# Sums of x in the projections, attention ahead of four products, stores on GpSimd, four embedding banks: one change to a hybrid decoder layer

## The chip, the cores and the metric

One core of one Trainium2 chip. The metric is the device time of one execution in microseconds (us); the median of repeated runs counts. The engines are named as in the profile: PE is TensorE (matmuls; PEld its weight loads), DVE is VectorE, ACT is ScalarE, POOL is GpSimd, SP is SyncE, which here only starts DMAs. "SPq" in a view is SP's queue of instructions, "PEclk" the granted share of TensorE's full clock.

## The reference

One layer with SEQ = 1024 tokens and D_MODEL = 2048, everything in fp32:

```python
h = rmsnorm(h_res, g_pre[i])
u = h @ w_in[i]
(gq, gk, gv, g_gate, g_lr, sq, sk, sv, s_gate) = jnp.split(u, offsets, axis=-1)
log_a = jax.nn.log_sigmoid(g_lr @ w_a2[i] + b_a[i]) / GLA_TAU
o_gla = gla_chunked(...)            # 4 heads, chunks of 64
o_gla = rmsnorm(o_gla, g_gla_head[i]) * jax.nn.silu(g_gate)
o_sb = stick_breaking(...)          # 8 heads, strictly causal
o_sb = o_sb * jax.nn.silu(s_gate)
mix = jnp.concatenate([o_gla, o_sb], axis=-1) @ w_out[i]
h_res = h_res + rmsnorm(mix, g_post[i])
gate = jax.nn.sigmoid(h_res @ w_ple_gate[i] + b_ple_gate[i])
h_res = h_res + gate * (p[i] @ w_ple_proj[i])
```

## The kernel before, in words

Everything lies transposed: features on the 128 partitions, tokens in two halves (hf 0 and 1) of 512. An fp32 product is made of three matmuls: each operand is split (lines 99 and 100) into a rounded high part and a low part, and hi·hi, lo·hi and hi·lo are added in one PSUM bank. High parts are made by ACT, low parts by DVE.

**Projections.** `dense` makes one unit of 128 columns of x·w_in for both halves: 16 k-steps of six matmuls, weights through `wload` (a load of 256 KB into one of two `raw` tiles, split into `hi` and `lo`, four tiles each). After each k-step `step()` advances generators, Python coroutines that hold the rest of the work cut into pieces: one piece of `urgent` (turning v by a DMA transpose), one of `beside`, and pieces of `jobs` at a rate (`rate[1]`). The jobs are here GLA's four heads (rate 1.0) and then the eight stick-breaking heads (rate 0.9). Results of projections lie in `u` tiles (12), attention's results go to DRAM, `o_d`. So the order of the work on each engine comes from where the generators are advanced, and from priorities (`tc.high_priority`), by which a scheduler draws loads and evictions forward.

**Tail.** The two gate columns of w_in (`w_gate`, silu's argument) aren't multiplied as a plain product but by a Strassen-Winograd scheme: seven products of halves in place of eight, with sums of x (S1 to S4), sums of weights and intermediate results (u, v). The first two of these products are made as 16 "small products" of 24 matmuls, through the same `raw` tiles, while attention's rest runs as `jobs`. The first eight (`keep_u1`) store their result in `u1_d`. The other eight (`gate_11`) load it again, load `o_d`, gate it and store `og_d`. Beside them, two generators in `beside`, `x_sets_2` and `x_sets_1`, make the sums of x that the next stage needs: they load quarters of x (`x_part`, 256 KB each), scale one by g_pre on ACT (L699), add or subtract on DVE (L700 and L714), split the sums S2 and S1 into PE's operands, and keep one sum for later (`sx_d`). The last `LAST_11` = 2 of the small products come after the attention pools have been closed, when the "mix" pool, whose tiles `wr` (4), `wh`, `wl` and `ar` (3 each) carry all that follows, has been opened.

**Wide stages.** From there blocks of eight "wide" products of 24 matmuls follow. In the loops, `wload2` loads 512 KB of weights into `wr` (L820), DVE makes sums of weights (L813, L816), `wsplit` splits them, and some weight sums are stored for a later stage (L992, L993; for w_out L1055, L1056). `staged` loads an operand into an `ar` tile (L802), `to_slot` splits it, and `fill` does that for a set. In order: S2 and S1 with sums of w_gate (16 products); x's second half (8); S3 (8), whose results `gate` turns into `og_d` of half 1; S4 (8), which does it for half 0, loading `o_d` for each pair of columns (L802) and storing `og_d` (L961). Then the same scheme for w_out: A11 (8), S2 and S1 (16), and so on, with the sums S1 to S4 of `og_d` made by `sums_12` (stores L879 and L884) and, during A11, by `last_sums`. Then the post norm, `stream` (which stores `h_d`), and the scheme once more for the embedding gate w_g, where `embed` makes two matmul groups of p·w_p into a PSUM bank of tag z (L1145 loads w_p), and `gated` (L1166 reads that bank) writes `out`.

All DMAs are started by SP, in the order in which it has them: an instruction that waits holds all behind it. PSUM's eight banks are dn 4, z 2, t 1, o 1. Tags t and o serve attention.

Of the kernel before, what the change touches and what calls it, by code (L numbers as in the profile page):

```python
# [18 lines left out]
P = 128  # L19
# [32 lines left out]
W = 2 * HT  # L52
KP = KT // 2
RATE_BG = 0.5
LAST_11 = 2


@with_exitstack
def layer(ctx, tc, xT, w_in, w_gate, w_lr, w_a2, b_a, g_pre, g_head, w_out, g_post,
# [64 lines left out]
    def part(t, k):  # L124
        return t[:, (k % 2) * HT:(k % 2 + 1) * HT]
# [22 lines left out]

    urgent, jobs, beside = deque(), deque(), deque()
    rate = [0.0, 0.0]  # L150

    def advance(queue):
        while queue:
# [100 lines left out]
    with tc.tile_pool(name="att", bufs=1, reuse_waits="tile") as ap:  # L254
# [379 lines left out]
        def low_rank(hf):  # L634
# [9 lines left out]
            A.activation(lrT[rows], z[rows], AF.Copy)  # L644
            V.tensor_tensor(lrT[rest], z[rest], f(lrT[rest]), op=ALU.subtract)

        rate[1] = RATE_GLA
# [35 lines left out]


        u1_d = [dram.tile([P, W], F32, name=f"u1_d{i}") for i in range(4)]
        sx_d = [dram.tile([P, W], F32, name=f"sx_d{i}") for i in range(4)]
        g_sets = {"S1": [], "S2": []}

        def g_of(k):
            return gpre_s[:, k:k + 1]  # L690

        def x_part(hf, k):
            t = at("u")
            dma2(t, part(xT[hf, k // 2], k))
            return t

        def x_sum(k):
            t, a = x_part(1, k + 8), x_part(1, k)
            A.activation(t, t, AF.Copy, scale=g_of(k + 8))  # L699
            V.scalar_tensor_tensor(t, a, g_of(k), t, op0=ALU.mult, op1=ALU.add)  # L700
            return t

        def x_set(name, hf, k, t, wides={}):
            if k % 2 == 0:
                wides[name] = act_wide(hf, k // 2)
            pair = tuple(part(x, k) for x in wides[name])
            split(*pair, t)
            g_sets[name].append(pair)

        def x_sets_2():  # L710
            for k in range(8):
                t, c = x_sum(k), x_part(0, k)
                yield 1
                V.scalar_tensor_tensor(c, c, g_of(k), t, op0=ALU.mult, op1=ALU.subtract)  # L714
                dma2(part(sx_d[k // 2], k), c)
                yield 1
                x_set("S2", 1, k, c)
                yield 1

        def x_sets_1():  # L720
            for k in range(8):
                t = x_sum(k)
                yield 1
                x_set("S1", 0, k, t)
                yield 1

        def small_product(a, src, evac):
            p = ps("dn")
# [45 lines left out]

    mp = ctx.enter_context(tc.tile_pool(name="mix", bufs=1, reuse_waits="tile"))
    late = [None]

    def mt(tag, bufs, n=W, dt=F32, name=None):
        pool = mp if tag in ("wr", "wh", "wl", "ar") else late[0]
# [6 lines left out]
    if True:  # L786
# [87 lines left out]
        def sums_12(rows, s1, s2):  # L874
            for i in rows:
                a, b, c = staged(og_d[0][i]), staged(og_d[0][i + 4]), staged(og_d[1][i])
                add(a, a, b)
                sub(c, c, a)
                dma2(s2_d[i], c)  # L879
                yield 1  # L880
                s2.append(to_slot(1, i, c))
                yield 1
                if s1 is None:
                    dma2(s1_d[i], a)  # L884
# [12 lines left out]
        rate[1] = RATE_BG  # L897

# [34 lines left out]
        def stream(hf, kp, c):  # L933
            x = staged(xT[hf, kp])
            for n in (2 * kp, 2 * kp + 1):
                V.scalar_tensor_tensor(part(c, n), part(c, n), gpost_s[:, n:n + 1], r[hf],
                                       op0=ALU.mult, op1=ALU.mult)
            add(c, c, x)
            dma2(h_d[hf][kp], c)
            yield 1  # L940


# [2 lines left out]
        def gate(n, hf, p, other):  # L945
# [15 lines left out]
            dma2(og_d[hf][n // 2], z)  # L961

        def times_g(t, kp):
            for k in (2 * kp, 2 * kp + 1):
                A.activation(part(t, k), part(t, k), AF.Copy, scale=g_of(k))

        def g_then(a, kp, b, op):
            for k in (2 * kp, 2 * kp + 1):
                V.scalar_tensor_tensor(part(a, k), part(a, k), g_of(k), part(b, k), op0=ALU.mult, op1=op)
            return a  # L970

        def make_x3(i):
            a, b = staged(xT[1, i]), staged(xT[0, i])
            times_g(b, i)
            return g_then(a, i, b, ALU.subtract)

        def make_x4(i):
            a, b = staged(xT[0, i + 4]), staged(sx_d[i])
            return g_then(a, i + 4, b, ALU.add)


        t2_d, t3_d = drams("g2_d", 8), drams("g3_d", 8)
# [2 lines left out]
        for j in range(8):  # L985
            with ahead():
                b11, t1, t2 = (wload2(w_gate[kh, nh, j]) for kh, nh in ((0, 0), (0, 1), (1, 1)))
                sub(t1, t1, b11)
                sub(t2, t1, t2)
                w2, w1 = wsplit(t2), wsplit(t1)  # L990
                add(b11, b11, t2)
                dma(t2_d[j], t2)  # L992
                dma(t3_d[j], b11)  # L993
            p = product(g_sets["S2"], w2)
            with soon():
                add(u(j), p, u(j))
            p = product(g_sets["S1"], w1)
            with soon():
                add(v(j), p, u(j))
        drain()  # L1000

        job(fill("S3", 1, make_x3))
        job(fill("S4", 2, make_x4))
        for j in range(8):
            with ahead():
                t4, t2 = wload2(w_gate[1, 0, j]), wload2(t2_d[j])
# [30 lines left out]
        for j in range(8):  # L1037
# [3 lines left out]
            with soon():  # L1041
                A.activation(u(j), p, AF.Copy)
                if j % 2:
                    dma2(m_d[j // 2], st_u[j // 2])
        drain()

        job(fill("S3", 0, both(og_d[0], og_d[1], sub)))
        for j in range(8):
            with ahead():
# [5 lines left out]
                dma(t2_d[j], t2)  # L1055
                dma(t3_d[j], b11)  # L1056
            p = product(sets["S2"], w2)
            with soon():
                add(u(j), p, u(j))
# [7 lines left out]
        for j in range(8):  # L1067
# [3 lines left out]
            with soon():  # L1071
# [2 lines left out]
                add(part(c, j), p, v(j))  # L1074
                add(u(j), p, u(j))
                if j % 2:
                    dma2(c_d[0][4 + j // 2], c)
                    squares(0, c)
        drain()

# [25 lines left out]
        for j in range(8):  # L1106
# [3 lines left out]
            with soon():  # L1110
# [1 line left out]
                    c = staged(m_d[j // 2])  # L1112
                add(part(c, j), p, part(c, j))
                if j % 2:
                    dma2(c_d[1][j // 2], c)
                    squares(1, c)
        drain()

# [9 lines left out]
        drain()  # L1128


        p_act, pw, res = {}, {}, {}

        def load_p(hf):
            raw = staged(pT[hf])
# [4 lines left out]
        def embed(n, hf):  # L1139
            def go():  # L1140
# [16 lines left out]
        def gated(n, hf, p, other, last=False):  # L1157
# [11 lines left out]
                dma2(part(out[hf, n // 2], n), t)  # L1169
            elif n % 2:  # L1170
                add(wide[key], wide[key], h)
                dma2(out[hf, n // 2], wide[key])

        def stream_1():
            norm(1)
# [43 lines left out]
        for j in range(8):  # L1219
            with ahead():  # L1220
# [4 lines left out]
                dma(t2_d[j], t2)  # L1225
            p = product(sets["S2"], w2)
            with soon():
                add(u(j), p, u(j))
# [101 lines left out]
```

## Time and profile before

| | |
|---|---|
| median of 3 runs | 2166.53 us (2165.53 to 2167.83) |
| the profiled execution | 2170.56 us |
| its span, first to last instruction | 2168.7 us |
| mean granted clock | 0.986 |
| busy PE, DVE, ACT, POOL | 2104.2, 1509.6, 882.5, 110.3 us |
| DMA | 354.92 MB, mean 164 GB/s |

Busy time is summed over an engine's instructions. In the groups and timelines an entry such as `dn<-ah,wh` is the output tile and the inputs, by the program's names; `L89 PE MATMUL` is the kernel's line, the engine and the operation. What stands after `<-` in an idle time is the engine, the tile and the line that ended it. A wait is put down to one releaser, the one that came last. The projections last until about 1115 us, the tail until 1244, the wide stages to the end.

### The profile page before, as it was taken

Reading aid. Unit: us, or ns where it says so; the run is one execution under the profiler, and the core shown is the slowest. Engines: PE = TensorE matmul, PEld = TensorE weight load, DVE = VectorE, ACT = ScalarE, POOL = GpSimd, SP = SyncE. Lnnn points to the kernel's source line nnn. Section 1 sums busy time; section 2 is a strip of 40 time slices with the busy share of each in tenths; the row PEclk is TensorE's granted clock in tenths of the full one; section 3 lists DMA queues with packets and bytes.
Section 4 is the critical chain, followed back from the end, with each engine's and each line's share of the span. In section 5 each row is a group of like instructions: output and inputs, shape, how many; then the busy total and the mean of one; then the engine's idle time right before and its main releaser. Section 6 shows DMA issues by size and latency. Waiting matters only on the chain.

```text
span 2168.7 us, 26868 instructions
## 1 busy us (share of the span) xinstructions
PE 2104.2 (97%) x9712; PEld 1716.6 (79%) x9712; DVE 1509.6 (70%) x2275; ACT 882.5 (41%) x1401; POOL 110.3 (5%) x228
## 2 busy tenths in 40 slices
PE   9999999999999999999999699999799999999998
PEld 6788888888888888888887588887588888778887
DVE  8557676666766666666677777886677787785765
ACT  7333333333455555544556323333233434322332
POOL 3000000000001110110100000000000000000000
PEclk9999999999999999999999899999799999999999
DMA  6212222221233334333359888778887686786763
GB/s 204 72 51 59 59 56 58 59 59 49 58 88 83 80 81 94 81 78 86 85 162 261 273 317 287 250 255 303 290 306 244 219 294 218 261 284 224 235 202 123
DMA packets 229669, 354.92 MB, mean 164 GB/s; under 512 B 124448, under 2 KB 129440, under 8 KB 229536
## 3 DMA queue, kind: packets, MB, share of 16 engines
q1 hardware_dynamic: 229536, 353.21, 51.9%
q8 instruction: 76, 1.25, 0.2%
q14 instruction: 57, 0.47, 0.1%
HBM read 257.19 MB, written 68.68 MB: 150 GB/s over the span
## 4 chain that ended last, share of the span: by engine, by line
PE 72%; DMA 13%; DVE 9%; issue 4%; ACT 2%; SPq 1%; DVEq 0%; POOL 0%; ACTq 0%
PE dn L89 63%; PE z L89 5%; DMA wr<-w_g 3%; PE t L89 2%; PE o L89 2%; DVE wl L100 2%; DMA u<-xT 1%; DMA E<-X 1%; DVE ev L813 1%; DMA ar<-og_d 1%; DMA og_d<-ev 1%; DMA xraw<-xT 1%; DMA ar<-xT 1%; DMA ar<-h_d 1%; DMA wr<-w_out 1%
## 5 line engine op out<-in xcount | busy, mean ns | idle before, releaser
L89 PE MATMUL dn<-ah,hi 128*128 128x512 f32 x1408 | 569.1, 404 | 0.2 <-ACT u L662 0.2
L89 PE MATMUL dn<-al,hi 128*128 128x512 f32 x1408 | 557.8, 396 | 0.3 <-DVE al L226 0.3
L89 PE MATMUL dn<-ah,lo 128*128 128x512 f32 x1408 | 557.8, 396 | 0.0
L89 PE MATMUL dn<-ah,wh 128*128 128x512 f32 x1216 | 478.1, 393 | 32.6 <-ACT ah L99 19.4
L89 PE MATMUL dn<-ah,wl 128*128 128x512 f32 x1216 | 476.7, 392 | 0.0
L89 PE MATMUL dn<-al,wh 128*128 128x512 f32 x1216 | 476.3, 392 | 0.1
L89 PEld LDWEIGHTS dn<-ah,hi 128*128 128x128 f32 x1408 | 265.8, 189 | 65.5 <-issue 2.8
L89 PEld LDWEIGHTS dn<-al,hi 128*128 128x128 f32 x1408 | 265.3, 188 | 65.4 <-DVE al L226 1.2
L89 PEld LDWEIGHTS dn<-ah,lo 128*128 128x128 f32 x1408 | 266.1, 189 | 54.3
L89 PEld LDWEIGHTS dn<-ah,wh 128*128 128x128 f32 x1216 | 230.5, 190 | 83.9 <-ACT ah L99 20.8
L99 ACT ACTIVATE wh<-wr 128x1024 fp32r<-128x1024 f32 x152 | 159.1, 1055 | 294.0 <-PE dn L89 140.1
L89 PEld LDWEIGHTS dn<-al,wh 128*128 128x128 f32 x1216 | 230.1, 189 | 50.1 <-DVE al L100 2.0
L89 PEld LDWEIGHTS dn<-ah,wl 128*128 128x128 f32 x1216 | 230.6, 190 | 48.4
L100 DVE TENSOR_TENSOR wl<-wr,wh 128x1024 fp32r<-128x1024 f32 x152 | 184.5, 1219 | 11.7 <-ACT wh L99 11.4
L99 ACT ACTIVATE hi<-raw 128x512 fp32r<-128x512 f32 x192 | 120.3, 627 | 154.8 <-PE dn L89 151.7
L100 DVE TENSOR_TENSOR lo<-raw,hi 128x512 fp32r<-128x512 f32 x192 | 133.7, 698 | 58.6 <-ACT hi L99 58.2
L305 ACT ACTIVATE X<-E 128x256 uint16<-128x256 uint16 (+2 forms) x96 | 80.9, 843 | 113.5 <-DVE E L578 99.9
L573 DVE TENSOR_TENSOR_SCAN X<-X 128x128 f32<-128x128 f32 (+2 forms) x96 | 98.1, 1022 | 35.4 <-POOL X L567 25.5
L99 ACT ACTIVATE ah<-ar 128x1024 fp32r<-128x1024 f32 x56 | 59.4, 1060 | 118.2 <-DVE ar L816 32.0
L588 DVE COPY v<-E 128x512 uint16<-128x512 uint16 (+1 forms) x160 | 64.1, 430 | 53.8 <-DMA E<-X 44.8
L816 DVE TENSOR_TENSOR wr<-wr,wr 128x1024 f32<-128x1024 f32 x48 | 58.7, 1223 | 50.6 <-DMA wr<-w_gate 23.9
L813 DVE TENSOR_TENSOR wr<-wr,wr 128x1024 f32<-128x1024 f32 x48 | 58.8, 1224 | 48.0 <-DMA wr<-w_g 31.0
(218 smaller groups left out, 2323.2 us busy)
## 6 DMA issues: line engine op xcount, KB each, us to landing
raw<-w_in SPq DMA_DIRECT2D x160, 256.0 KB, 2.7
wr<-w_g SPq DMA_DIRECT2D x64, 512.0 KB, 4.3
wr<-w_out SPq DMA_DIRECT2D x56, 512.0 KB, 4.6
wr<-w_gate SPq DMA_DIRECT2D x40, 512.0 KB, 4.7
ar<-og_d SPq DMA_DIRECT2D x36, 512.0 KB, 5.1
ar<-h_d SPq DMA_DIRECT2D x36, 512.0 KB, 5.0
g_d<-wr SPq DMA_DIRECT2D x32, 512.0 KB, 3.2
wr<-g_d SPq DMA_DIRECT2D x32, 512.0 KB, 4.9
```

Of the source, the lines that this page charges most:

```text
L89: PE.matmul(o, lhsT, rhs, start=start, stop=stop)
L99: A.activation(hi, src, AF.Copy)
L100: (eng or V).tensor_tensor(lo, src, f(hi), op=ALU.subtract)
L305: A.activation(pl.rearrange("p (two n) -> p two n", two=2), src.bitcast(U16)[:, :2 * n].rearrange("p (n two) -> p two n", two=2), AF.Copy)
L573: V.tensor_tensor_scan(rev, rev, rev, initial=kq[:, n:n + 1], op0=ALU.mult, op1=ALU.bypass)
L588: V.tensor_copy(to[:, :, :m, j], w[:, :, 2 * g:2 * g + m])
L813: V.tensor_tensor(dst, a, b, op=ALU.add)
L816: V.tensor_tensor(dst, a, b, op=ALU.subtract)
```

## The change

- **Sums of x.** A generator `x_sums` is put into `beside` at unit 5 of the projections. Its 32 pieces, one every `PACE_QKV` = 15 k-steps, load the quarters of x (four loads of 256 KB for each of eight k), make S1, S3, S2 and S4 and store each in DRAM (`sx_d`), all in `u` tiles. In the tail, `x_set` now only loads S2 and S1 and splits them (16 loads of 256 KB), one piece every `PACE_TAIL` = 4 steps, and S3 and S4 are filled by plain loads later. The scalings, sums and stores of x_sum in the tail are gone.
- **Attention.** In the tail its jobs are advanced at `RATE_TAIL` = 1.1 pieces a step instead of 0.9, and `LAST_11` is 4 instead of 2: four small products come after attention's pools are closed.
- **Stores.** From the wide stages on, stores are started by GpSimd (`store = G.dma_start`) instead of SP.
- **last_sums.** It makes row 3 of S1 and S2 first and loads rows 0 to 2 of S1 after that. Before, it was the other way round.
- **Embedding.** Its banks go round "ztzo": four PSUM banks instead of the two of tag z.

```diff
 RATE_BG = 0.5
-LAST_11 = 2
+RATE_TAIL = 1.1
+LAST_11 = 4
+PACE_QKV, PACE_TAIL = 15, 4
...
     def step():
         advance(urgent)
-        advance(beside)
+        pace[0] += 1
+        if pace[0] % pace[1] == 0:
+            advance(beside)
...
+            for k in range(8):
+                g, g8 = gpre_s[:, k:k + 1], gpre_s[:, k + 8:k + 9]
+                s1, a21 = x_part(1, k + 8), x_part(1, k)
+                A.activation(s1, s1, AF.Copy, scale=g8)
+                V.scalar_tensor_tensor(s1, a21, g, s1, op0=ALU.mult, op1=ALU.add)
+                keep("S1", k, s1)
+                yield 1
+                a11 = x_part(0, k)
+                A.activation(a11, a11, AF.Copy, scale=g)
+                V.scalar_tensor_tensor(a21, a21, g, a11, op0=ALU.mult, op1=ALU.subtract)
+                keep("S3", k, a21)
+                yield 1
+                V.tensor_tensor(a11, a11, s1, op=ALU.subtract)
+                keep("S2", k, a11)
+                yield 1
+                a12 = x_part(0, k + 8)
+                V.scalar_tensor_tensor(a12, a12, g8, a11, op0=ALU.mult, op1=ALU.add)
+                keep("S4", k, a12)
+                yield 1
...
+            if u == 5:
+                beside.append(x_sums())
...
-        beside.append(x_sets_2())
+        while beside:
+            advance(beside)
+        rate[1], pace[1] = RATE_TAIL, PACE_TAIL
+        beside.append(x_set("S2", 1))
         for j in range(8):
             small_product(x_act[0][:8], w_gate[0, 0, j], keep_u1(j))
-        beside.append(x_sets_1())
+        while beside:
+            advance(beside)
+        beside.append(x_set("S1", 0))
...
         def last_sums(s2):
             s1 = []
+            yield from sums_12((3,), s1, s2)
+            sets["S2"] = parts(s2)
             for i in range(3):
-                s1.append(to_slot(2, i, staged(s1_d[i])))
-                yield 1
-            yield from sums_12((3,), s1, s2)
-            sets["S1"], sets["S2"] = parts(s1), parts(s2)
+                s1.insert(i, to_slot(2, i, staged(s1_d[i])))
+                yield 1
+            sets["S1"] = parts(s1)
...
             V.tensor_tensor(z, z, g, op=ALU.mult)
-            dma2(og_d[hf][n // 2], z)
+            store(og_d[hf][n // 2], z)
...
-        job(fill("S3", 1, make_x3))
-        job(fill("S4", 2, make_x4))
+        job(fill("S3", 1, plain(sx_d["S3"])))
+        job(fill("S4", 2, plain(sx_d["S4"])))
...
-                z = ps("z")
+                z = ps(next(pw_tags))
```

SP now has 877 instructions instead of 956, and POOL has 107 more; DVE and ACT have about as many as before, and PE's are the same in number. The new lines shift the line numbers: L116 becomes L118 (`raw`), L308 L313 (transposes), L820 L837 (`wr`), L802 L819 (`ar`), L615 L620 (`o_d`), L753 to L760 L764 to L771 (gate_11).

**SP, end of the tail.** What SP starts around the first four loads of wide weights (`wr`); `st` are the loads of u1, `raw` weights of small products, `og_d` the stores of gated small products. Before:

```order
L760 DMA og_d_0_696<-u_11336 128x512
L984 DMA st_11511<-u_d_10196 128x1024
L760 DMA og_d_0_696<-u_11389 128x512
L615 DMA o_d_1_693<-o_11404 128x512
L984 DMA st_11512<-u_d_10197 128x1024
L984 DMA st_11513<-u_d_10198 128x1024
L820 DMA wr_11598<-w_gate 128x1024
L820 DMA wr_11600<-w_gate 128x1024
L820 DMA wr_11602<-w_gate 128x1024
L820 DMA wr_11669<-w_gate 128x1024
L753 DMA ar_11450<-u_d_10199 128x512
L754 DMA ar_11451<-o_d_0_681 128x512
```

Now:

```order
L771 DMA og_d_0_695<-u_11274 128x512
L620 DMA o_d_1_693<-o_11326 128x512
L118 DMA raw_11492<-w_gate 128x512
L771 DMA og_d_0_695<-u_11343 128x512
L118 DMA raw_11521<-w_gate 128x512
L837 DMA wr_11658<-w_gate 128x1024
L118 DMA raw_11539<-w_gate 128x512
L837 DMA wr_11660<-w_gate 128x1024
L837 DMA wr_11662<-w_gate 128x1024
L837 DMA wr_11729<-w_gate 128x1024
L764 DMA ar_11416<-u_d_10358 128x512
L765 DMA ar_11417<-o_d_0_680 128x512
```

The loads of `st` no longer stand ahead of the four `wr`, and attention's last store (`o_d`) is followed by raw weights of small products. On PE, in the same place, 23 matmuls of small products (`dn`) stand between attention's last matmul and the first wide one before, and 102 now.

**SP, the A11 stage.** What SP starts around the load of `o_d` for the last gate; `g_d` are stores of weight sums, `m_d` of results, `s_d` of sums of og. Before:

```order
L820 DMA wr_13709<-w_out 128x1024
L802 DMA ar_13155<-og_d_1_704 128x1024
L1055 DMA g_d_11579<-wr_13642 128x1024
L1056 DMA g_d_11587<-wr_13638 128x1024
L1044 DMA m_d_11525<-st_13231 128x1024
L820 DMA wr_13711<-w_out 128x1024
L820 DMA wr_13713<-w_out 128x1024
L879 DMA s_d_11528<-ar_13155 128x1024
L884 DMA s_d_11521<-ar_13151 128x1024
L1055 DMA g_d_11580<-wr_13713 128x1024
L1056 DMA g_d_11588<-wr_13709 128x1024
L802 DMA ar_13220<-o_d_0_685 128x1024
```

Now:

```order
L837 DMA wr_13658<-w_out 128x1024
L819 DMA ar_13240<-o_d_0_685 128x1024
L837 DMA wr_13660<-w_out 128x1024
L819 DMA ar_13266<-og_d_0_697 128x1024
L837 DMA wr_13662<-w_out 128x1024
L837 DMA wr_13729<-w_out 128x1024
L819 DMA ar_13268<-og_d_0_701 128x1024
L819 DMA ar_13270<-og_d_1_705 128x1024
L837 DMA wr_13731<-w_out 128x1024
L819 DMA ar_13301<-s_d_11579 128x1024
L837 DMA wr_13733<-w_out 128x1024
L819 DMA ar_13321<-s_d_11580 128x1024
```

The load of `o_d` moves up past three weight loads and all the stores, and the loads of S1's rows (`ar` from `s_d`) stand behind the loads for row 3 of S2.

**SP, in the projections.** One of the 32 new pieces; `E` from `X` are transposes. Before:

```order
L116 DMA raw_2151<-w_in 128x512
L116 DMA raw_2212<-w_in 128x512
L308 DMA_TRANSPOSE E_1911<-X_1909 128x8x128
L308 DMA_TRANSPOSE E_1985<-X_1983 128x8x128
L116 DMA raw_2268<-w_in 128x512
L116 DMA raw_2331<-w_in 128x512
```

Now:

```order
L118 DMA raw_2246<-w_in 128x512
L313 DMA_TRANSPOSE E_1941<-X_1939 128x8x128
L313 DMA_TRANSPOSE E_2015<-X_2013 128x8x128
L658 DMA u_2121<-xT 128x512
L662 DMA S4x_d_740<-u_2121 128x512
L118 DMA raw_2309<-w_in 128x512
L118 DMA raw_2372<-w_in 128x512
```

A load of x and the store of the sum that is made of it stand, one right behind the other, between the transposes and the next raw weights.

More of the change, by code (lines that the diff above doesn't have):

```diff
@@ L150, in layer @@
     rate = [0.0, 0.0]
+    pace = [0, PACE_QKV]
     def advance(queue):
@@ L645, in low_rank, with x_sums, x_part, keep @@
             V.tensor_tensor(lrT[rest], z[rest], f(lrT[rest]), op=ALU.subtract)
+        sx_d = {n: [dram.tile([P, W], F32, name=f"{n}x_d{i}") for i in range(4)] for n in ("S1", "S2", "S3", "S4")}
+        def x_sums():
+            def x_part(hf, k):
+                t = at("u")
+                dma2(t, part(xT[hf, k // 2], k))
+                return t
+            def keep(name, k, t):
+                dma2(part(sx_d[name][k // 2], k), t)
+            for k in range(8):
[17 more added lines that the diff above has]
+                yield 1
         rate[1] = RATE_GLA
@@ L685, in layer, with x_set @@
         u1_d = [dram.tile([P, W], F32, name=f"u1_d{i}") for i in range(4)]
-        sx_d = [dram.tile([P, W], F32, name=f"sx_d{i}") for i in range(4)]
         g_sets = {"S1": [], "S2": []}
[L689 to L710, printed above, removed]
+        def x_set(name, hf):
             for k in range(8):
-                t, c = x_sum(k), x_part(0, k)
+                t = at("u")
+                dma2(t, part(sx_d[name][k // 2], k))
                 yield 1
-                V.scalar_tensor_tensor(c, c, g_of(k), t, op0=ALU.mult, op1=ALU.subtract)
-                dma2(part(sx_d[k // 2], k), c)
-                yield 1
[L717 to L725, printed above, removed]
+                if k % 2 == 0:
+                    wides = act_wide(hf, k // 2)
+                pair = tuple(part(x, k) for x in wides)
+                split(*pair, t)
+                g_sets[name].append(pair)
         def small_product(a, src, evac):
@@ L776, in layer @@
     late = [None]
+    store = G.dma_start
     def mt(tag, bufs, n=W, dt=F32, name=None):
@@ L878, in sums_12 @@
                 sub(c, c, a)
-                dma2(s2_d[i], c)
+                store(s2_d[i], c)
                 yield 1
@@ L883, in sums_12 @@
                 if s1 is None:
-                    dma2(s1_d[i], a)
+                    store(s1_d[i], a)
                 else:
@@ L938, in stream @@
             add(c, c, x)
-            dma2(h_d[hf][kp], c)
+            store(h_d[hf][kp], c)
             yield 1
@@ L1043, in layer @@
                 if j % 2:
-                    dma2(m_d[j // 2], st_u[j // 2])
+                    store(m_d[j // 2], st_u[j // 2])
         drain()
@@ L1114, in layer @@
                 if j % 2:
-                    dma2(c_d[1][j // 2], c)
+                    store(c_d[1][j // 2], c)
                     squares(1, c)
@@ L1171, in gated @@
                 add(wide[key], wide[key], h)
-                dma2(out[hf, n // 2], wide[key])
+                store(out[hf, n // 2], wide[key])
         def stream_1():
@@ L1224, in layer @@
                 w2, w1 = wsplit(t2), wsplit(t1)
-                dma(t2_d[j], t2)
+                store(t2_d[j], t2)
             p = product(sets["S2"], w2)
```

26 lines of the change are left out of this document (6 added, 20 removed).

## Prediction

> **What bounds the kernel now.** I read the page's first part, then PE's waits, then windows of 30 us. TensorE is the bound, and what can be won is what it idles or runs at half clock.
>
> ```profile
> PE 2104.2 (97%) x9712; PEld 1716.6 (79%) x9712; DVE 1509.6 (70%) x2275; ACT 882.5 (41%) x1401; POOL 110.3 (5%) x228
> ```
>
> The waits of PE (engine, line, tile waited for; us in total, times, longest), under the line with the span, show that nearly all the idle time has few causes.
>
> ```profile
> core 0 of [0], span 2168.7 us
> engine line waited for: us in total, times, longest us
> PE dn L89 <- ACT ah L99: 19.4, 3, 11.9
> PE dn L89 <- ACT wh L99: 13.3, 4, 10.6
> PE t L89 <- DVE s L100: 7.3, 3, 3.8
> PE z L89 <- DVE ev L1166: 5.0, 1, 5.0
> PE z L89 <- ACT E L563: 3.9, 1, 3.9
> PE z L89 <- DVE pl L100: 2.6, 3, 1.2
> ```
>
> PE's idle time is 2168.7 - 2104.2 = 64.5 us. Where it lies is told by windows (columns: the stretch, busy us and instructions of PE, PEld, DVE, ACT and POOL, granted clock, DMA share, GB/s):
>
> ```profile
> core 0: us, PE busy (x) PEld busy (x) DVE busy (x) ACT busy (x) POOL busy (x), PEclk, DMA share, GB/s
> 1140.00:1170.00 30.00, 25.95 (x113) 20.72 (x112) 22.55 (x42) 17.80 (x35) 2.21 (x7) 0.92 0.92 256
> 1170.00:1200.00 30.00, 27.71 (x126) 22.54 (x125) 26.03 (x44) 21.83 (x39) 3.21 (x5) 0.97 0.95 277
> 1200.00:1230.00 30.00, 24.39 (x106) 18.97 (x105) 24.97 (x44) 13.54 (x24) 0.00 (x0) 0.94 0.74 230
> 1230.00:1260.00 30.00, 19.28 (x71) 14.99 (x70) 17.82 (x20) 5.27 (x6) 0.00 (x0) 0.77 0.87 315
> 1260.00:1290.00 30.00, 30.00 (x134) 24.85 (x133) 21.92 (x23) 7.79 (x10) 0.00 (x0) 1.00 0.86 329
> 1500.00:1530.00 30.00, 16.16 (x63) 12.00 (x61) 16.01 (x14) 5.69 (x7) 0.00 (x0) 0.83 0.93 328
> 1530.00:1560.00 30.00, 23.13 (x79) 17.39 (x80) 17.46 (x16) 9.23 (x9) 0.00 (x0) 0.77 0.77 266
> 1860.00:1890.00 30.00, 27.88 (x122) 22.32 (x121) 24.05 (x28) 10.84 (x15) 0.00 (x0) 1.00 0.79 269
> 1890.00:1920.00 30.00, 24.97 (x98) 20.06 (x97) 24.78 (x27) 8.24 (x11) 0.00 (x0) 0.89 0.83 287
> ```
>
> Three places, each idle time plus busy time x (1 - clock), which is about what the low clock adds:
> - A, 1140 to 1260, the tail: idle 4.05 + 2.29 + 5.61 + 10.72 = 22.7; clock 2.1 + 0.8 + 1.5 + 4.4 = 8.8; together 31.5. The waits for wh (10.6), s (7.3) and E (3.9) make up its idle time.
> - B, 1500 to 1560, the first S2 and S1 products of w_out: idle 13.84 + 6.87 = 20.7, clock 2.8 + 5.3 = 8.1; 28.8. Here are the waits for ah.
> - C, 1860 to 1920, the embedding in the last gate stage: idle 2.12 + 5.03 = 7.2, clock 2.7; 9.9. The wait for L1166 is here.
>
> Together 70.2 us: if all went and nothing came, the profiled execution's 2170.6 would be 2100. One matmul takes 30/134 = 0.224 us, so a product of 24 takes 5.4 us and a stage of eight 43.
>
> **Sums of x moved into the projections, and A.** The tail's rows in the line groups from 1115 to 1245:
>
> ```profile
> L700 DVE SCALAR_TENSOR_TENSOR u<-u,c,u 128x512 f32<-128x512 f32 x15 | 11.2, 748 | 4.2 <-DMA u<-xT 2.5 <-ACT u L699 1.4
> L699 ACT ACTIVATE u<-u,c 128x512 f32<-128x512 f32 x15 | 10.8, 719 | 7.2 <-DMA u<-xT 7.2
> ```
>
> Gone from the tail are 16 vector sums of this form and eight of the same size at L714, which I price alike, 24 by 0.75 us (18 us), 16 scalings by 0.72 us (11.5 us), 24 of 40 loads and all eight stores of 256 KB. VectorE was busy 22.55 + 26.03 + 24.97 = 73.6 of the 90 us in which s and E came late. A quarter less work there should take most of those 11.2 us of idle, but attention is also asked to run at 1.1 steps for 0.9, so it needs what is left sooner; I leave 5 us.
>
> The 10.6 us wait for wh is one of order. SyncE's issues and TensorE's first wide matmul (in brackets how long it stood before it, and for whom):
>
> ```profile
> 1230.14 1.75 SPq L984 DMA_DIRECT2D st<-u_d  x2
> 1232.01 2.84 SPq L820 DMA_DIRECT2D wr<-w_gate  x4
> ```
>
> ```profile
> 1243.74 0.80 PE L89 MATMUL dn<-ah,wh 128*128 128x512 f32 x1 [10.57 <-ACT wh L99]
> ```
>
> The first wide weights were issued at 1232.0, behind loads of st and attention's last store, and the first wide matmul ran 11.7 us later. In the order of before 23 matmuls of the last product stand between attention's last matmul and it: 5.2 us of cover, and 10.6 were lacking. Now 102 stand there, 23 us, and SyncE has the four wr loads ahead of the st loads. The first wr still stands behind the gate store of product 3. That store's chain (load of o_d and u, four vector operations, a sigmoid) I put at 4.5 to 8 us after its product; with 11.7 more the weights are there 16.2 to 19.7 us after product 3, and four products last 21.5. So that wait goes, with 2 to 5 us to spare. A leaves 5 of idle and 1 of clock: 31.5 to 6, a gain of 25.5 (bounds: 14, if attention's 11.2 and its clock stay, and 31.5).
>
> What it puts elsewhere: 32 steps, each with one load or two, one or two vector operations and a store. In the projections SyncE waits for buffers of weights, so it is early:
>
> ```profile
> SPq L116 <- DVE lo L100: 413.1, 114, 13.2
> ```
>
> That is 3.6 us each time. The hi and lo tiles hold four pairs, each of 24 matmuls (5.4 us): a lead of up to 21.5 us. A step blocks SyncE at its store for load plus sum, 4.3 + 0.75 = 5 us (the load's row is below), and the raw loads and transposes queued behind it come so much later; the lead covers that for weights. For transposes, which attention waits for, I have no row that shows the slack: between 0 and 6 us in all, I take 2, being nearer to the covered weights. S3 and S4 become eight plain loads of 512 KB in place of 16 loads and 32 scalings and sums; A, B and C hold all but 2.7 us of the waits for wh and ah, so TensorE loses next to nothing in those stages, and I cost it at nothing.
>
> **Stores by GpSimd, the order of last_sums, and B.** TensorE's first matmul of B, and SyncE's issues:
>
> ```profile
> 1519.91 0.79 PE L89 MATMUL dn<-ah,wh 128*128 128x512 f32 x1 [7.04 <-ACT ah L99]
> ```
>
> ```profile
> 1527.82 0.45 SPq L802 DMA_DIRECT2D ar<-o_d  x1
> ...
> 1535.27 0.32 SPq L961 DMA_DIRECT2D og_d<-ev  x1
> ```
>
> This load belongs to the last gate. The A11 stage ended at 1519.9 - 7.0 = 1512.9, and the gate's product a stage of 43 us earlier, at about 1470: the load is 58 us late. In the order of before it stands behind stores of weight sums (g_d), of sums (s_d) and of m_d, each of which waits for its own VectorE or TensorE work, and behind weight loads that wait for buffers. Behind it, in a chain, come gate, store, load, subtraction, split, and TensorE's 11.9 us wait. Now the stores are off SyncE, and that load stands between weight loads only. Rows for the chain (DMA: us to landing; groups: mean ns):
>
> ```profile
> ar<-og_d SPq DMA_DIRECT2D x36, 512.0 KB, 5.1
> ...
> u<-xT SPq DMA_DIRECT2D x40, 256.0 KB, 4.3
> ...
> ar<-o_d SPq DMA_DIRECT2D x12, 512.0 KB, 4.7
> og_d<-ev SPq DMA_DIRECT2D x12, 512.0 KB, 3.9
> ...
> ar<-s_d SPq DMA_DIRECT2D x7, 512.0 KB, 5.6
> ```
>
> ```profile
> L99 ACT ACTIVATE ah<-ar 128x1024 fp32r<-128x1024 f32 x56 | 59.4, 1060 | 118.2 <-DVE ar L816 32.0
> ...
> L816 DVE TENSOR_TENSOR wr<-wr,wr 128x1024 f32<-128x1024 f32 x48 | 58.7, 1223 | 50.6 <-DMA wr<-w_gate 23.9
> ```
>
> The weight load ahead of it waits for a buffer that is free about the end of the fifth of eight products, 3 x 5.4 = 16.2 us before the stage's end. From there: load 4.7, two VectorE operations 2.4, store 3.9, load 5.1, two operations 2.4, split 1.1 = 19.6. Row 3 of S2 is ready 3.4 us after the stage's end and wanted after three quarters of a product, 4.0: no wait. But S1's rows 0 to 2 are now loaded after it: about 5.6 and a split of 2.3 behind it, 3.4 + 7.9 = 11.3, wanted at 5.4: 6 us of idle, more if the weight loads between them wait. With the clock (8.1 on 20.7) that is 8; I take 13 for what stands between. B goes from 28.8 to 13, a gain of 15.8 (bounds 0 and 28.8).
>
> On GpSimd a store waits behind other stores; an m_d store waits for its product and holds the og_d store behind it. POOL is idle there (0.00 in these windows), and SyncE's own issue takes 0.32 to 0.45 us. No row shows a store from GpSimd: it may land earlier, having less ahead of it, or later; bounds -4 to +6 over the chains that TensorE waits for, taken at 2. By the Trainium skill (DMA: Bandwidth & Descriptors, "Latency and other measured facts") the first byte comes after about 0.6 us by hardware descriptors and about 1 us by software ones; no run here shows it yet, and 0.4 us over the two stores in that chain would be 0.8.
>
> **Four embedding banks, and C.** The embedding product (tag z, two banks) waited 5.0 us for L1166 to free its bank. Tags t and o are free in these stages, so two more products may be outstanding and that wait goes, with its low clock. The small waits for pl (2.6 in all) stay: C goes from 9.9 to 2.4, a gain of 7.5 (bounds 5 and 9.9).
>
> **Sum.** 25.5 + 15.8 + 7.5 - 2 - 2 = 44.8. The profiled execution, 2170.6, becomes 2125.8. It stood 4.0 above the median of before (2166.5), so the median becomes 2121.8, say 2122.
>
> **Rivals.**
> 1. *Slower: the sums of x starve the projections.* SyncE issues in order; each of 32 steps holds it about 5 us at a store, and the u tiles stay taken meanwhile, which the projections' evictions need. If TensorE pays p us at each, the cost is 32p; it eats the gain from p = (44.8 + 2)/32 = 1.46 us. With 2.5 us, half of a block, it is 80, for 2 in the sum: 2200. For it: the 5 us block and twelve u tiles. Against: 3.6 us to spare at 114 loads and four pairs in stock. Chance 0.08.
> 2. *The stores gain nothing.* If B is late through transfers (DMA share 0.93 and 0.77), or weight buffers hold the o_d load as the stores did, B stays at 28.8: 2122 + 15.8 = 2138. For it: the DMA share. Against: the o_d load alone came 58 us late. Chance 0.17. Beside it stands the rule of the Trainium skill (DMA: Bandwidth & Descriptors, "Issuing engines are not separate DMA queues") that starting transfers from several engines only saves the sequencer's time for issuing. By that rule this rival would hold; the rows agree that issuing is short (0.32 to 0.45 us), but they also show what the rule does not count, a load held behind a store that still waits for its data.
> 3. *Attention at 1.1 starves.* VectorE must do the rest of attention in a shorter time; the waits for s and E stay, A gains 14: 2122 + 11.5 = 2133. For it: VectorE is the busiest beside TensorE there. Against: 18 us less on it. Chance 0.15.
>
> **How the numbers follow.** Forecast 0.54, rivals 0.08, 0.17 and 0.15, and 0.06 for other outcomes (an operation that the trace of before doesn't show taking most of the gain: 0.04 no change, 0.02 slower). About 0.2% (4.3 us) is what a measurement of this kernel can tell from no change. Rivals 2 and 3 are faster still, even together (2149). So faster 0.86, same 0.04, slower 0.10. The range goes from 2104 (all three places nearly closed, costs at nothing) to 2150 (rivals 2 and 3 together).
>
> **What would show it.** Right: PE's wait for L1166 gone; the wait for wh at the wide start under 2 us, with the wr loads issued before the last small product starts; PE idle in the tail about 5 us; waits for ah at the first w_out products falling to some 9 us, on S1's rows rather than S2's; the o_d load within 40 us of its product; PE's projections as full as before. Wrong: new PE waits for hi, s or u below 1115, or SyncE waiting at the sums' stores with the clock row under 9 there (rival 1); B's idle near 20 with the o_d load early (rival 2); waits for s over 10 us before the last four products (rival 3).

## The result and the profile after

The changed kernel takes 2187.5 us, median of 4 runs (2186.4 to 2200.1), against 2167.2 (2165.5 to 2170.9) before on the same chip: ratio 1.0105, 95% interval 1.0065 to 1.0144. It is slower by about 20 us where 45 us less were forecast. The profiled execution took 2186.4 us, its span is 2184.7.

The page's line of busy times, to be set against 2104.2 of before:

```profile
PE 2111.6 (97%) x9712; PEld 1716.9 (79%) x9712; DVE 1501.9 (69%) x2267; ACT 874.6 (40%) x1393; POOL 164.9 (8%) x330
```

TensorE idles 2184.7 - 2111.6 = 73.1 us where it was 64.5. PE's waits have changed their kind:

```profile
PE dn L91 <- ACT ah L101: 17.6, 2, 16.7
PE dn L91 <- DVE wl L102: 14.9, 12, 2.5
PE t L91 <- DVE pl L102: 6.0, 2, 4.7
PE z L91 <- DVE pl L102: 4.3, 3, 2.1
PE dn L91 <- DVE ev L830: 3.7, 1, 3.7
```

The long wait for wh (10.6) and the one for L1166 (5.0) are gone and those for s are small, as forecast. In their place stand twelve short waits for wl, waits for pl and one for ev: what VectorE makes comes late in many places where before it did not. The windows of A, B and C, in the columns of the prediction:

```profile
1140.00:1170.00 30.00, 28.85 (x139) 23.59 (x137) 21.82 (x44) 19.81 (x40) 2.83 (x10) 1.00 0.67 182
1170.00:1200.00 30.00, 27.13 (x127) 21.70 (x128) 22.68 (x40) 15.24 (x27) 1.61 (x2) 1.00 0.85 237
1200.00:1230.00 30.00, 26.76 (x116) 21.00 (x115) 22.07 (x31) 12.16 (x21) 1.26 (x2) 1.00 0.79 278
1230.00:1260.00 30.00, 30.00 (x133) 24.54 (x132) 23.75 (x29) 6.34 (x8) 2.13 (x4) 1.00 0.95 336
1260.00:1290.00 30.00, 26.43 (x101) 20.67 (x101) 19.05 (x20) 6.66 (x7) 3.19 (x6) 0.89 0.78 278
1500.00:1530.00 30.00, 13.26 (x57) 10.45 (x55) 19.04 (x17) 7.69 (x9) 5.29 (x10) 0.76 0.98 340
1530.00:1560.00 30.00, 29.10 (x117) 23.14 (x117) 21.81 (x22) 10.27 (x10) 2.13 (x4) 0.90 0.85 304
1860.00:1890.00 30.00, 23.17 (x90) 17.82 (x90) 20.63 (x25) 9.34 (x12) 2.12 (x4) 0.94 0.79 274
1890.00:1920.00 30.00, 27.53 (x111) 21.91 (x112) 26.35 (x31) 9.95 (x13) 2.65 (x5) 0.94 0.83 277
```

The tail is nearly full, but 1260 to 1290, full before, now idles 3.6 us at a granted clock of 0.89; C is emptier than before.

The matmuls come in the same number, so the programs can be lined up: the table takes the start of the first matmul of each stage from PE's timeline. "Projections" ends with dn matmul 3840 of 4224; wide products are counted from 0, and four last 21.8 us when nothing is missing. First column: the length before; the others: how much longer (+) or shorter each profiled execution was. The columns behind "after" are experiments, below.

| stage | before, us | after | e1 | e2 | e3 | e4 | e8 |
|---|---|---|---|---|---|---|---|
| projections | 1109.9 | +4.6 | +4.6 | -0.7 | +4.1 | +2.2 | +2.9 |
| tail, to the first wide product | 133.8 | -19.2 | -17.0 | -1.0 | -17.5 | -16.7 | -15.6 |
| products 0 to 3 | 25.3 | -3.1 | +11.4 | -0.1 | -2.2 | +10.4 | +2.8 |
| 4 to 23 | 108.8 | +11.1 | +2.4 | +4.6 | +4.3 | +1.6 | +1.1 |
| 32 to 35 (gate, half 0) | 23.4 | +4.0 | -0.1 | +5.6 | +8.9 | +4.8 | +0.4 |
| 48 to 51 (B) | 49.8 | -6.8 | +5.5 | -12.0 | -13.8 | -4.8 | -12.4 |
| 88 to 103 | 87.9 | +7.9 | 0.0 | +5.2 | +1.0 | +6.4 | 0.0 |
| 104 to 115 (C) | 87.5 | +7.0 | -9.3 | +8.8 | +6.5 | +6.2 | -8.3 |
| 116 to the end | 236.9 | +7.6 | -0.6 | +9.1 | +6.3 | +3.4 | +4.3 |
| the rest | 305.5 | +3.1 | 0.0 | +3.2 | +6.2 | +1.0 | +3.9 |

A column is one execution, and executions differ by some us: e1's is the fastest of its ten (2167.3, median 2173.8), e3's the slowest of its ten (2174.3, median 2169.9), and that of the kernel before, 2170.6, is 3 us above its median. In e2 and e5, whose tails no edit touches, the tail is 1.0 and 3.0 us shorter than in it, so about that much of a gain in the tail may be spread.

Some 1.6 of the projections' 4.6 us arise in the first 80 us, ahead of the change. So A gained 19.2 + 3.1 = 22.3 us. More than that was lost again behind it: 7.0 in C, where a gain was forecast, and 33.7 in stages for which the prediction had no term. What moved in these stages is the engine that starts the stores.

### The profile page after: what moved, and what is told of

It reads as the page before. It is cut to its first block, busy times and chain, and to the rows that moved or that the text cites. A ratio compares the mean times of both kernels' runs of the same rounds, so it can differ in the third digit from the quotient of the medians.

```text
span 2184.7 us, 26969 instructions
## 1 busy us (share of the span) xinstructions
PE 2111.6 (97%) x9712; PEld 1716.9 (79%) x9712; DVE 1501.9 (69%) x2267; ACT 874.6 (40%) x1393; POOL 164.9 (8%) x330
## 4 chain that ended last, share of the span: by engine, by line
PE 61%; issue 24%; DMA 8%; DVE 4%; POOL 2%; ACT 2%; SPq 0%; POOLq 0%; DVEq 0%; ACTq 0%
PE dn L91 51%; PE z L91 5%; PE t L91 2%; PE o L91 2%; DMA wr<-w_g 1%; DMA E<-X 1%; DMA g_d<-wr 1%; DMA ar<-h_d 1%; DMA wr<-w_gate 1%; DVE wl L102 1%; DMA xraw<-xT 1%; DVE wr L833 1%; DMA u<-S2x_d 0%; DMA u<-S1x_d 0%; DVE ev L830 0%
## 5 line engine op out<-in xcount | busy, mean ns | idle before, releaser
L91 PE MATMUL dn<-ah,wh 128*128 128x512 f32 x1216 | 479.6, 394 | 25.4 <-ACT ah L101 17.6
```

The costliest lines, as they stand in the source:

```text
L91: PE.matmul(o, lhsT, rhs, start=start, stop=stop)
```

## The experiments

Theory 1: a store from GpSimd lands later than one in SyncE's order, the tiles of the rings (a ring is the few buffers that one kind of tile goes round: wr, ar, ev) come free that much later, and with them weight loads, sums and TensorE. Theory 2, the rival: the losses come from the other parts. "Timed" is a median, with the ratio to runs of the kernel before on the same chip (medians 2165.8 for e1 to e4, 2167.9 for e5 to e8, 2166.8 for e9 and e10).

**e1, stores on SyncE.**

```diff
-    store = G.dma_start
+    store = dma2
```

> The changed kernel with its stores back on SyncE; all else as changed. Theory 1 (a store from GpSimd lands later, and the wr, ar and ev tiles come free that much later; weight loads and VectorE's sums then come late for TensorE): the losses of the wide stages after 1250 us (9 us in the w_gate block, 2, 4, 2, 8, 10, 4 and 4 us in later ones, some 40 in all) go, and B may get its 7 us back: about 2187 - 40 + 7 = 2154, between 2140 and 2160. Theory 2 (the losses come from the other parts: plain fills, the order of last_sums, four banks): about 2187, no less than 2180, and the same stages are long.

Timed 2173.8 (2167.3 to 2181.1, 10 runs), ratio 1.0030 (1.0015 to 1.0046). The losses after product 4 went, as theory 1 has it, C is 9.3 us shorter than before, and the kernel won 14 us over the changed one. But it isn't faster than before, a miss for the number: two gains went as well, and PE's waits name them:

```profile
PE dn L91 <- ACT ah L101: 27.7, 3, 22.4
PE dn L91 <- DVE ar L766: 9.0, 3, 5.9
PE dn L91 <- DVE st L830: 5.1, 1, 5.1
```

L766 is the eviction of the last four small products and st the loads of u1: both loads now stand behind SyncE's stores of weight sums, and the dn banks, four, stay full until they come. The tail's gain of 17.0 is spent on products 0 to 3 (+11.4). And B, with stores in SyncE's order and last_sums turned round, waits 22.4 us for one operand.

**e2, only the stores moved**, on the kernel before: each `dma` and `dma2` that the change turned into `store`, and nothing else.

> The kernel before with only its stores of the wide stages moved to GpSimd. Theory 1: the losses appear without the other parts, 2167 + 40 - 7 = about 2200, and the waits of SyncE's weight loads for g_d to land rise from 19 us to over 80. Theory 2: within 10 us of 2167.

Timed 2193.1 (2191.1 to 2195.0), ratio 1.0123 (1.0103 to 1.0143): slower by 27 us, with only this part. The waits of SyncE's loads for a landed store of weight sums rose as expected. Here is that wait in the kernel before, among SyncE's waits at those stores themselves (L992, L993, L1055, L1056), and then in e2:

```profile
SPq L992 <- DVE wr L816: 40.5, 8, 6.6
...
SPq L1055 <- DVE wr L816: 28.6, 8, 5.7
...
SPq L820 <- DMA g_d<-wr: 19.4, 17, 3.6
...
SPq L1056 <- DVE wr L813: 9.4, 8, 2.6
...
SPq L993 <- DVE wr L813: 8.0, 8, 1.4
```

```profile
SPq L821 <- DMA g_d<-wr: 111.1, 29, 9.3
```

But this rise says little: before, SyncE stood at the stores until VectorE's sums were ready, and together that was 40.5 + 28.6 + 9.4 + 8.0 + 19.4 = 105.9 us. The clearer sign is VectorE's own wait for a tile that a store still reads (`st`, into which it adds while h_d is stored from it), before and here:

```profile
DVE st L813 <- DMA h_d<-st: 5.4, 4, 2.0
```

```profile
DVE st L814 <- DMA h_d<-st: 16.1, 3, 7.3
```

It is 4.3 to 5.7 us in every run in which SyncE starts h_d (before, e1, e5, e6, e8, e10), 15.3 to 16.6 in every run in which GpSimd does (the changed kernel, e2, e4, e7, e9), and 8.3 in e3, where ScalarE does. The same wait for og_d goes from 4.4 to 6.4 up to 8.2 to 10.1, and 7.5 in e3. Theory 2 falls as the main cause. One thing comes with the move that no run takes apart: SyncE's loads and VectorE's steps also stand in another order in the program. B by itself gained 12.0, more than in the changed kernel.

**e3, stores by ScalarE.**

```diff
-    store = G.dma_start
+    store = A.dma_start
```

> The changed kernel with its stores started by ScalarE, that is from a hardware queue, but not in SyncE's order. If the late landing comes of GpSimd's own way of starting (theory 1a), stores land as from SyncE (out about 3.8 us instead of 6.3, h_d 4.2 instead of 6.5) and the weight loads' wait for g_d is short again; the time then depends on what ScalarE's activations lose by waiting behind stores, 2150 to 2190. If it comes of a second queue sharing the DMA engines with the loads (theory 1b), the landing stays near 6 us and the time at 2187 or more.

Timed 2169.9 (2165.1 to 2174.3, 10 runs), ratio 1.0017 (1.0004 to 1.0029). That is 18 us less than the changed kernel, so it is a miss for theory 1b, which had 2187 or more. The landing of stores (last column, median us from issue) of before, after and e3:

```profile
out<-ev SPq DMA_DIRECT2D x15, 512.0 KB, 3.8
...
og_d<-ev SPq DMA_DIRECT2D x12, 512.0 KB, 3.9
...
h_d<-st SPq DMA_DIRECT2D x8, 512.0 KB, 4.3
...
h_d<-ar SPq DMA_DIRECT2D x8, 512.0 KB, 4.1
```

```profile
out<-ev POOLq DMA_DIRECT2D x15, 512.0 KB, 6.3
...
og_d<-ev POOLq DMA_DIRECT2D x12, 512.0 KB, 4.0
...
h_d<-st POOLq DMA_DIRECT2D x8, 512.0 KB, 6.4
...
h_d<-ar POOLq DMA_DIRECT2D x8, 512.0 KB, 6.9
```

```profile
out<-ev ACTq DMA_DIRECT2D x15, 512.0 KB, 5.6
...
og_d<-ev ACTq DMA_DIRECT2D x12, 512.0 KB, 3.8
...
h_d<-st ACTq DMA_DIRECT2D x8, 512.0 KB, 6.6
...
h_d<-ar ACTq DMA_DIRECT2D x8, 512.0 KB, 7.0
```

The stores of out and h_d land about as late from ScalarE as from GpSimd, which is a miss for theory 1a; og_d's land as before from all three. Over all 102 stores the mean landing is 4.1 us before, 5.3 after and 5.1 from ScalarE. So most of the later landing is not GpSimd's way of starting: it belongs to a store that runs beside SyncE's loads instead of in line with them. That the loads share the DMA engines with it is the likely reason, and not shown apart. But later landing can't be the whole cost, or e3 would have stayed at 2187. Against the changed kernel it is 6.8 us shorter in products 4 to 23, 7.0 in B and 6.9 in 88 to 103, and no run says how much of that is GpSimd's start and how much the other order of the instructions. What the traces show of GpSimd's own part is small. In the first w_gate block g_d landed in 3.1 us before, 4.4 after and 3.5 from ScalarE, and a POOL start comes later and takes longer. DVE's last sum and the store of it, after and e3:

```profile
1248.65 1.23 DVE L830 TENSOR_TENSOR wr<-wr,wr 128x1024 f32<-128x1024 f32 x1
...
1250.17 0.53 POOL L993 DMA_DIRECT2D g_d<-wr  x1 [0.73 <-DVE wr L830]
```

```profile
1252.21 1.22 DVE L830 TENSOR_TENSOR wr<-wr,wr 128x1024 f32<-128x1024 f32 x1
...
1253.47 0.33 ACTq L993 DMA_DIRECT2D g_d<-wr  x1
```

GpSimd starts 0.29 us after the sum's end (1249.88) and needs 0.53 us; ScalarE starts 0.04 us after it and needs 0.33.

**e4, only the weight sums' stores back on SyncE** (40 of 102): `store(t2_d[j], t2)` and `store(t3_d[j], b11)` become `dma(...)`.

> The changed kernel with only the stores of weight sums (40 of the 102) back on SyncE; og_d, s_d, m_d, c_d, h_d and out stay on GpSimd. Theory 1: the w_gate block loses nothing (9 to 11 us back) and the w_out block 2 us and the w_g block 4 us less; the losses at S4 and in the embedding stages, which wait for og_d, c_d and h_d, stay: about 2187 - 16 = 2171. Theory 2: 2187.

Timed 2185.9 (2184.8 to 2196.0), ratio 1.0105 (1.0072 to 1.0139): nothing won, where 16 us were expected. The table shows both halves: products 4 to 23 get 9.5 us back, as expected, and products 0 to 3 lose 13.5, the wait that e1 has there. I had not counted that.

**e5, only the four banks**, on the kernel before: `z = ps(next(pw_tags))`.

> The kernel before with only the four embedding banks. Theory 1 (this part does what was forecast, as the stages of the changed kernel with SyncE's stores show: 8 us between products 104 and 112): 2166 - 8 = 2158 and no wait for L1166. Theory 2 (the banks shift the wait to the small splits of w_p, so nothing is won): 2166, with waits for pl of 5 us or more.

Timed 2164.7 (2159.1 to 2168.4, 11 runs), ratio 0.9985 (0.9975 to 0.9995): a gain of 1 to 5 us by the timed runs, of 8 expected. The profiled execution, 2160.8, is one of the fastest; in it the wait for L1166 is gone and products 104 to 115 are 9.0 us shorter, while 2.0 us are given back from 116 on. The part does what was forecast at its place. Why less than that reaches the median is not shown.

**e6, only the sums of x and the tail** (stores on SyncE, old last_sums, two banks).

> The kernel before with only the sums of x in the projections and the tail's changes (rate, LAST_11, plain fills): stores on SyncE, the old order in last_sums, two banks. Theory 1 (the tail's gain is spent in the next products, since the gates of the last four small products load behind SyncE's stores of weight sums, and hold all four dn banks): wide start about 12 us earlier, but level with before by the fourth wide product; 2166 + 3 = 2169, with waits for L766 and st of 10 us or more in all. Rival (the tail's gain of over 15 us stays and the rest of the changed kernel with SyncE's stores took it): about 2152.

Timed 2165.2 (2162.5 to 2170.5, 10 runs), ratio 0.9994 (0.9984 to 1.0005): no change. The tail is 20.8 us shorter, products 0 to 3 13.5 longer, the projections 4.2 longer, with the waits for L766 (9.5 us) and st (6.2) of e1. Theory 1's account holds.

**e7, the old order in last_sums**, else as changed.

> The changed kernel with the old order in last_sums (rows 0 to 2 of S1 loaded first). Theory 1 (the new order puts S1's loads behind row 3 of S2, while the old one has them done early): the first four products of w_out take about 38 us instead of 43, as they do where only the stores are on GpSimd; 2187 - 5 = 2182. Rival (the new order helps): 2187 or more.

Timed 2183.1 (2178.4 to 2187.8), ratio 1.0069 (1.0051 to 1.0087), against 1.0105 for the changed kernel: the intervals overlap, so the gain of some 4 to 8 us is likely, not certain (5 were expected). B is 9.8 us shorter than before, where the new order has 6.8. In e1 against e6, with stores on SyncE, the order alone makes 5.5 against 0.1.

**e8, a mix.** As e1, with the old last_sums, and GpSimd only for what SyncE's order would hold up:

```diff
+    far = G.dma_start
...
-            dma2(st_u[i], u1_d[i])
+            far(st_u[i], u1_d[i])
...
-                store(t2_d[j], t2)
+                (far if j < 3 else store)(t2_d[j], t2)
...
-                store(s2_d[i], c)
+                far(s2_d[i], c)
```

`t3_d` goes like `t2_d` in the w_gate block, both with `j < 2` in the w_out block; `s1_d` and `m_d` go like `s2_d`.

> A mix: the changed kernel with its stores on SyncE and the old last_sums, but by GpSimd: the loads of u1 into st, the stores of weight sums for the first three products pairs of w_gate and the first two of w_out, and the stores s_d and m_d. Theory 1 (GpSimd pays where SyncE's order holds up a load that is wanted at once, and costs where a ring waits for the landing): the tail's 17 us and B's 12 and the banks' 8 are kept, 3 us go in the projections and 2 in the w_gate block: 2166 - 32 = 2134, between 2128 and 2145. Theory 2 (every store from GpSimd costs): 2166 or more.

Timed 2148.2 (2147.5 to 2149.7), ratio 0.9907 (0.9892 to 0.9922): 20 us faster than before and 39 than the changed kernel, though 14 short of my number and outside its range. The page's busy line, beside a span of 2147.8, and PE's largest waits:

```profile
PE 2102.5 (98%) x9712; PEld 1712.4 (80%) x9712; DVE 1502.8 (70%) x2267; ACT 874.7 (41%) x1393; POOL 121.8 (6%) x253
```

```profile
PE dn L91 <- ACT wh L101: 5.0, 2, 3.3
PE dn L91 <- ACT ah L101: 4.7, 3, 2.7
PE dn L91 <- ACT ar L769: 4.3, 1, 4.3
```

B and C keep their gains, and A keeps 15.6 - 2.8 = 12.8 of its 22.3 us. Missing are 3.6 us in the tail and 5.9 in products 0 to 3 against the changed kernel, with the wait for L769 above, a gate of the last small products, and 4.3 and 3.9 us from 116 on and in the rest.

**e9, the mix with og_d and h_d on GpSimd**, 28 stores.

> The mix with og_d's and h_d's stores on GpSimd as well. Theory 1 (these hold ev and ar tiles until they land, and what waits for the tile stands ahead of other work): products 32 to 36 take 4 to 6 us longer, 88 to 96 some 3 and 104 to 112 some 10; 2148 + 18 = 2166. Rival (in the changed kernel the losses came of all 102 stores together, not of these): 2148 to 2152.

Timed 2173.5 (2167.2 to 2181.6, 10 runs), ratio 1.0032 (1.0016 to 1.0048): 25 us more than the mix. Against the mix, products 32 to 35 are 4.7 us longer, 88 to 103 2.8, 104 to 115 20.0, in an execution that is one of the faster of its ten. The first two are as expected, the last is twice that. Two of PE's waits:

```profile
1426.74 0.47 PE L91 MATMUL dn<-ah,wh 128*128 128x512 f32 x1 [4.84 <-DVE ev L831]
```

```profile
1849.18 0.80 PE L91 MATMUL t<-ph,pl 128*128 128x512 f32 x1 [4.57 <-DVE pl L102]
```

The second can be followed back on VectorE. A step there adds into `st` once the store of h_d from it has landed; first in the mix, then here, with the split of w_p that TensorE waited for:

```profile
1830.82 1.23 DVE L831 TENSOR_TENSOR st<-st,ar 128x1024 f32<-128x1024 f32 x1 [1.61 <-DMA h_d<-st]
```

```profile
1837.08 1.22 DVE L831 TENSOR_TENSOR st<-st,ar 128x1024 f32<-128x1024 f32 x1 [6.91 <-DMA h_d<-st]
...
1848.71 0.42 DVE L102 TENSOR_TENSOR pl<-pr,ph 128x256 fp32r<-128x256 f32 x1
```

VectorE stands 6.9 us for the landing where it stood 1.6, and then has a queue of steps ahead of the split. So C's loss is h_d's for the most part. By its place the first loss is og_d's (VectorE's wait for its landing is 8.2 us here and 5.7 in the mix); that 88 to 103 belong to h_d rests on the place alone.

**e10, the mix with c_d and out on GpSimd**, 23 stores.

> The mix with c_d's and out's stores on GpSimd as well. Theory 1: c_d holds ar and ev tiles too, so products 88 to 96 take some 4 us longer, and out holds ev in the last stages, some 4 us at 136 to 148; 2148 + 8 = 2156. Rival (only h_d and og_d matter): 2148.

Timed 2158.6 (2155.5 to 2166.6, 10 runs), ratio 0.9965 (0.9953 to 0.9976): 10 us more than the mix. Products 88 to 103 are 2.9 us longer and 116 to the end 6.1 (104 to 115 3.0) in the profiled execution, which is the slowest of its ten, 8 us above their median; 2156 was expected.

## Why the prediction was wrong

- **A** was right: 31.5 to 6 was forecast (25.5), 22.3 came. The wait for wh at the wide start went (1.35 us is left, for an eviction), and the waits for s and E fell from 11.2 us to under 7. What I had not seen is that this rests on the stores: with those of weight sums on SyncE (e1, e4, e6) products 0 to 3 take 10 to 13.5 us longer than before, with full dn banks. Rival 3 did not occur. The lower bound of 14 comes out as 31.5 - 11.2 - 4.4 = 15.9 if the clock terms of the three windows are taken, which changes nothing.
- **The projections** were right in kind: of 4.6 us about 3 come after the sums begin (2 forecast); in the other runs with these sums the stage is 2 to 5 us longer than before. Rival 1 did not occur.
- **B** was mis-sized: 15.8 forecast, 6.8 came. TensorE's wait there, in the changed kernel:

```profile
1529.15 0.79 PE L91 MATMUL dn<-ah,wh 128*128 128x512 f32 x1 [16.74 <-ACT ah L101]
```

The load of o_d did come early, issued at 1501.8 rather than 1527.8. But the chain that I put at 19.6 us took 27.4 up to this matmul: the loads in it took nearer 7 us than 5, and stores and VectorE's steps came later. The turned order of last_sums was a loss of 3 to 5.5 us (e1 against e6, e7 against the changed kernel) where I took it as given. With the old order and stores from GpSimd B does gain 10 to 12 (e2, e7, e8). The order is no loss by itself, for with stores from ScalarE it stands beside a gain of 13.8 (e3).
- **C** was right as a mechanism: 7.5 forecast, 9.0 to 9.3 in e1 and e5's profiled executions (1 to 5 us by e5's timed runs). In the changed kernel it became a loss of 7.0, mostly by h_d's stores (e9): VectorE stood 16.6 us in all until they landed. The small waits for pl, which were to stay at 2.6, came to 10.3.
- **The step that failed** is "bounds -4 to +6 over the chains that TensorE waits for, taken at 2", for stores from GpSimd. I counted the chain of B and took the other stores as free because POOL is idle. They cost not POOL's time but the tile's: a store holds its tile until it lands, 5.3 us instead of 4.1 on the mean of all 102 and 6.4 to 6.9 instead of 4.1 to 4.3 for h_d, and what writes the tile next waits, be it a load or VectorE. VectorE's wait for h_d and og_d shows this; for the weight sums in products 4 to 23, e4 shows that their stores make the loss, and the way there is argued. Summed over products 4 to the end and set against e1, whose edit differs by the stores alone, the changed kernel loses 8.7 us (4 to 23), 4.1 (32 to 35), 7.9 (88 to 103), 16.3 (104 to 115), 8.2 (116 on) and 3.1 (the rest): 48. It wins 14.5 at products 0 to 3 and 12.3 in B: 27. Net about 21 us in these stages of the two executions (whose spans differ by 19.1), and 14 by the timed medians. Later landing is not the whole of it, for e3 with much the same landing is 18 us faster: what else the stores from GpSimd cost stays open.
- **Rival 2**, that the stores gain nothing, put them at zero and not at a loss. Its sign, B's idle time near 20 us with the o_d load early, nearly came: 16.74 + 0.90 = 17.6 us at a DMA share of 0.98 and 0.85. But its cause did not, since B gains 10 to 12 us with GpSimd's stores and the old order. The rule that stood beside it, from the Trainium skill (DMA: Bandwidth & Descriptors, "Issuing engines are not separate DMA queues"), is that another engine only saves issue time. The runs differ from it both ways: moving the stores alone made B 12.0 us shorter and the kernel 27 us longer (e2). A rival with the losses' mechanism, on the other side, is what was missing. By the Trainium skill (DMA: Bandwidth & Descriptors, "Latency and other measured facts") the first byte comes after about 1 us by software descriptors and about 0.6 by hardware ones, an estimated 0.4 us between them. The runs don't show it as a fixed step: between GpSimd and ScalarE lie 0.2 us on the mean of all 102 stores (5.3 and 5.1), 0.9 for g_d in the first w_gate block (4.4 and 3.5), and for h_d ScalarE is no earlier (6.6 and 7.0 against 6.4 and 6.9).

**What stays open**: why a store lands later from either other queue, by 1.0 to 1.3 us on the mean and by 2 to 3 for h_d and out (sharing with SyncE's loads is likely, not shown); why e3 lost so much less than the changed kernel (whether VectorE's work slows a start on GpSimd was not tested); and how much of each loss comes of the landing and how much of the other order of loads and steps that the move brings. In C the split of w_p stands 11.6 us behind the step that waits for h_d in e9, and 7.5 in the mix.

## What to carry to other kernels

Moving stores off a queue that issues in order was worth here the loads that they held up, and only those: look for a load that is wanted at once behind a store that still waits for its data. Before moving the others, ask which tile each store holds until it lands, how deep that ring is, and what stands behind the load or the vector step that waits for it. A wait that appears on a queue may only have moved there from the instruction ahead, so add both up. A part that gains in one stage may rest on another part of the same change, so each needs a run alone and a run without it.

## What the runs showed of the hardware

The same 512 KB stores of out and h_d landed in about 4 us (3.8 to 4.3) in line with the loads on SyncE's queue, and in 5.6 to 7.0 us from ScalarE's or GpSimd's, with the loads running beside them; og_d's landed in 3.8 to 4.0 from all three. Over all 102 stores the mean was 4.1 us from SyncE, 5.1 from ScalarE and 5.3 from GpSimd. GpSimd's instruction that starts a store took 0.53 us and began 0.29 us after the data was ready; ScalarE's took 0.33 and began 0.04 us after it. SyncE's took 0.32.
